# RWKV heads' transposes, inverse levels and chain outputs in fewer, larger steps, and working memory given back in smaller pieces

## The chip, the cores and the metric

The kernel runs on one core of a Trainium2 chip. The metric is the device time of one execution in microseconds; of a kernel, the median of its runs. The core has a matrix engine (TensorE, PE in the profile), a vector engine (VectorE, DVE), a scalar engine (ScalarE, ACT), GpSimd (POOL) and SyncE (SP), which run their own instruction streams and wait for one another by semaphores. SBUF is the working memory, PSUM holds what PE writes.

## What is computed

One layer of a decoder for 288 tokens (256 of a prompt, 8 sequences of 4 new tokens), all in float32:

```
h = RMSNorm_pre(x);  [p_rwkv | lru_x | lru_gate | q | k | v] = h @ W_in
y = concat(RWKV7(p_rwkv), RGLRU(lru_x, lru_gate), DilatedWindowAttn(q, k, v)) @ W_out
x = x + RMSNorm_post(y)
x = x + RMSNorm_post2(relu(RMSNorm_pre2(x) @ W1)^2 @ W2)
```

The width is 2048, the inner width of the feed-forward part 8192. RWKV7 has 8 heads of 64 with a matrix state, scanned along the tokens; the RG-LRU is a gated linear recurrence over 512 channels behind a convolution of width 4; the attention has 8 heads of 128 and, for the 32 new tokens, caches of keys and values of 2048 positions, of which 896 are used. The new states, keys and values are outputs too.

## The kernel before

**The weight stream.** All weights come as 380 chunks of 512 KB on SP's queue, into four slots (`w32`). Float32 precision is had by splitting: ACT rounds a chunk to its high half (`ring_h`, L393), DVE subtracts it and keeps the low half (`ring_l`, L394), into three slots each, and each product is three products of PE, high by high (L429), low by high (L430), high by low (L431), with 288 tokens as columns. These 128x288 products are called mains here. A chunk is 24 mains; the split of chunk i needs the slot of chunk i - 3. The chunks run in the order W_in (92 chunks, to about 480 us), W_out in four passes (32 chunks, to about 600 us), then the feed-forward part with 256.

**The other work.** RWKV, LRU and attention are written as Python generators in a list `gens`. After each chunk `pump(budget)` asks each generator for its next step, in the order of their priorities and of the list, until a budget is spent; a step that finds its operands missing yields nothing. A tile scheduler then places the step's instructions into each engine's stream. So on PE the main products of a chunk are interrupted by groups of small products of some step, and the list, the budget and the scheduler settle where.

**The generators of this change.** `gen_tok` (L786) transposes B, K and V of a half of the RWKV heads, `gen_mats` (L875) does the last doubling levels of the inverse of a triangular matrix, four heads at a time, `gen_chain` (L937) runs over the chunks of 64 tokens and updates the state Z, `gen_gn` (L1130) is the group norm, `gen_rwkv_sample` (L1027) does the new tokens, `gen_lru` (L1192) the recurrence, `gen_tables` (L1324) the position biases, `gen_sample_scores` (L1363), `gen_sample_soft` (L1431) and `gen_sample_pv` (L1458) the attention of the new tokens with the caches.

**The working memory.** `arena` hands out pieces of two SBUF tiles, `arx` and `ar1`; a generator that gets no piece yields and asks again. PE's small products write to five banks of PSUM (`banks`). The caches stream through `streams`, two buffers that are the halves of the tile `arm`. K loads (L1377, 1792 columns) and V loads (L1474, 2048 or 1536 columns) are issued on POOL's queue as soon as a buffer is free; `more_streams` (L359) adds up to two more buffers from the arena late in the phase. One V step takes two loads and has 28 products (L1496).

Of the kernel before, what the change touches and what calls it, by code (L numbers as in the profile page):

```python
# [11 lines left out]
AF = mybir.ActivationFunctionType  # L12
# [5 lines left out]
NT = NP_ + NS  # L18
# [293 lines left out]
def build(tc, A, O):  # L312
    nc = tc.nc
    sy, dv, ac, po, pe = nc.sync, nc.vector, nc.scalar, nc.gpsimd, nc.tensor
    with ExitStack() as ctx:
# [38 lines left out]
        arena = Arena([arx, ar1])  # L354
        facc = arm.rearrange("p (k t) -> p k t", k=KT)
        streams = [arm[:, 0:2304], arm[:, 2304:4608]]
# [186 lines left out]
        lora = arena.get(2, 512)  # L543
# [22 lines left out]
        def gen_prenorm():  # L566
# [12 lines left out]
            sy.dma_start(out=lora, in_=A["lora"].rearrange("p (a b) -> p a b", a=2))  # L579
# [81 lines left out]
        def gen_rwkv(hf):  # L661
# [6 lines left out]
            for f in range(2):  # L668
# [3 lines left out]
                pe.matmul(out=b0[:, :NT], lhsT=lora[0:64, 0, fs], rhs=mw[0:64], start=True, stop=True)  # L672
                pe.matmul(out=b1[:, :NT], lhsT=lora[64:128, 0, fs], rhs=mw[64:128], start=True, stop=True)
# [3 lines left out]
                yield 1.0  # L677
            half_up(LW, -0.5 * CDEC)
# [59 lines left out]
            gens.append(gen_tok(R, "B", BK[:, 0]))  # L738
            gens.append(gen_tok(R, "K", BK[:, 1]))
# [27 lines left out]
            gens.append(gen_tok(R, "V", MV))  # L767
# [18 lines left out]
        def gen_tok(R, name, src):  # L786
            for j in range(2):
                t = yield from aw(256, top=True)
                b, = yield from bk(1)
                for f in range(2):  # L790
                    pe.transpose(b[:, 128 * f:128 * f + 128], src[:, f, 128 * j:128 * j + 128], ident)
                ac.activation(out=t, in_=b[:, 0:256], func=AF.Copy)
                banks.put(b)
                R[name + str(j)] = t
                yield 0.25
# [79 lines left out]
        def gen_mats(hf, j):  # L875
            R = RS[hf]
            while "MA%d" % j not in R:
                yield 0
            MT = R["MA%d" % j]
            i64 = cbv("i64")  # L880
            i64b = i64.unsqueeze(1).to_broadcast([128, 4, 64])
# [4 lines left out]

            rc = (slice(0, 64), slice(64, 128))
# [5 lines left out]
            T, Q = R["TQ"][:, 4 * j:4 * j + 4], R["TQ"][:, 8 + 4 * j:12 + 4 * j]  # L893
            for l in range(4, 6):
                b, = yield from bk(1)
                for h in range(4):
                    for r in rc:
                        pe.matmul(out=v4(b)[r, h], lhsT=XT[r, h], rhs=T[r, h], start=True, stop=True)  # L898
                dv.tensor_tensor(out=Gp, in0=v4(b), in1=i64b, op=ALU.add)
                banks.put(b)  # L900
                if l < 5:
                    dv.tensor_tensor(out=XT, in0=MT[:, :, 0], in1=lvl(l + 1), op=ALU.mult)
                yield 0.65
# [4 lines left out]
                for h in range(4):  # L908
                    for r in rc:
                        if l < 5:  # L910
                            pe.matmul(out=v4(bT)[r, h], lhsT=Q[r, h], rhs=Gp[r, h], start=True, stop=True)
                        pe.matmul(out=v4(bQ)[r, h], lhsT=Gp[r, h], rhs=Q[r, h], start=True, stop=True)
                if l < 5:
                    ac.activation(out=T, in_=v4(bT), func=AF.Copy)
                    banks.put(bT)
                ac.activation(out=Q, in_=v4(bQ), func=AF.Copy)
                banks.put(bQ)
                yield 1.3 if l < 5 else 0.65
            arena.put(XT, Gp)
            while "V%d" % j not in R:  # L920
                yield 0
            VT = R["V%d" % j]
            AV = yield from aw(4, 64, top=True)
            b, = yield from bk(1)
            for h in range(4):
                e, f = h // 2, h % 2
                for r in rc:
                    pe.matmul(out=v4(b)[r, h], lhsT=MT[r, h, 1], rhs=VT[r, 128 * f + 64 * e:128 * f + 64 * e + 64],
                              start=True, stop=True)
            ac.activation(out=AV, in_=v4(b), func=AF.Copy)  # L930
            banks.put(b)
            arena.put(MT)
            yield 0.65
            R["AV%d" % j] = AV
            R["Q%d" % j] = Q

        def gen_chain(hf):  # L937
# [13 lines left out]
            for g in range(4):  # L951
# [7 lines left out]
                if g:  # L959
                    be = yield from bk(2)  # L960
                    for f in range(2):
                        for e in range(2):
                            re = slice(64 * e, 64 * e + 64)
                            pe.matmul(out=be[e][r, 64 * f:64 * f + 64], lhsT=AR[re, 0, f, tok], rhs=Z[re, f],
                                      start=True, stop=True)
                    for e in range(2):
                        dv.tensor_tensor(out=RH[r, 2 * e:2 * e + 2], in0=v2(be[e])[r], in1=AV[r, 2 * e:2 * e + 2], op=ALU.add)
                    banks.put(*be)
                    yield 0.35
# [38 lines left out]
                if g:  # L1008
                    bZ, = yield from bk(1)
                    for f in range(2):  # L1010
                        for e in range(2):
                            re = slice(64 * e, 64 * e + 64)
                            pe.matmul(out=bZ[re, 64 * f:64 * f + 64], lhsT=Z[re, f], rhs=AR[re, 1, f, tok],
                                      start=True, stop=True)
                    dv.tensor_tensor(out=yv, in0=v2(bZ), in1=yv, op=ALU.add)
                    banks.put(bZ)
# [836 lines left out]
```

## Time and profile before

| | |
|---|---|
| median of 3 runs | 1447.4 us (1447.09 to 1448.56) |
| profiled execution | 1447.71 us, of which the span is 1445.6 |
| mean granted clock of PE | 0.989 |
| PE busy | 1412.0 us, 98% of the span |
| DVE busy | 836.5 us, 58% |
| ACT busy | 600.2 us, 42% |
| POOL busy | 63.3 us, 4% |
| HBM | 190 GB/s over the span |

The span goes from the first to the last instruction of the trace. Busy time of PE is the time in which it has any product in flight; a group of small products among mains counts as busy like the mains themselves. The granted clock is the share of TensorE's full speed in a stretch; its two levels are 1.2 and 2.4 GHz. A wait is the idle time of an engine before an instruction, with what ended it.

### The profile page before, as it was taken

The numbers are of one execution on the slowest core, as the hardware profiler recorded it, in microseconds if no ns is written. First come the engines' busy times: TensorE is split into PE (matmuls) and PEld (weight loads), VectorE is DVE, ScalarE is ACT, GpSimd is POOL, SyncE is SP. The second block draws the span as 40 slices with busy tenths as digits, with TensorE's granted clock in tenths as the row PEclk, the third lists the DMA queues.
The fourth block names the chain that finished last, engine by engine and source line by source line (L and its number), as shares of the span: only waits on it lengthen the run. The fifth ranks groups of instructions, "written<-read, shape, count | busy, mean of one in ns | idle before, by whom it ended". The sixth has DMA issues, their size and how long they took to land.

```text
span 1445.6 us, 27979 instructions
## 1 busy us (share of the span) xinstructions
PE 1412.0 (98%) x11730; PEld 1340.2 (93%) x11730; DVE 836.5 (58%) x1431; ACT 600.2 (42%) x870; POOL 63.3 (4%) x127
## 2 busy tenths in 40 slices
PE   8999999899999999999999999999999999999995
PEld 8899778777878999999999999999999999999995
DVE  7796476645686756795533455544455444555555
ACT  7433422333352533664433344333344333444442
POOL 2101010210001100000000000000000000000000
PEclk9999999999999999999999999999999999999998
DMA  8546566676678774344444444444444445444442
GB/s 299 181 152 209 187 240 239 223 271 241 217 292 331 290 286 162 131 148 161 170 164 165 170 162 163 172 161 167 169 161 165 171 161 169 167 161 165 171 162 79
DMA packets 86047, 276.62 MB, mean 191 GB/s; under 512 B 22385, under 2 KB 26017, under 8 KB 83873
## 3 DMA queue, kind: packets, MB, share of 16 engines
q1 hardware_dynamic: 75136, 212.23, 42.6%
q0 software_dynamic: 9920, 60.83, 11.2%
q8 instruction: 92, 1.51, 0.4%
q10 hardware_dynamic: 864, 1.77, 0.4%
q14 instruction: 35, 0.28, 0.1%
HBM read 267.97 MB, written 6.84 MB: 190 GB/s over the span
## 4 chain that ended last, share of the span: by engine, by line
PE 82%; issue 7%; DMA 6%; DVE 4%; POOL 1%; ACT 0%; SPq 0%; POOLq 0%; DVEq 0%; ACTq 0%
PE mm L429 25%; PE mm L431 25%; PE mm L430 25%; DMA arm<-in_vc 2%; DMA arm<-in_kc 2%; PE bt L1409 1%; DVE ring_l L394 1%; PE bt L1496 1%; DMA ar<-in_vc 1%; DMA w<-in_w_in 0%; DVE arm L1830 0%; DMA do<-ar 0%; DVE arx L1831 0%; DVE hl L548 0%; PE bt L898 0%
## 5 line engine op out<-in xcount | busy, mean ns | idle before, releaser
L394 DVE TENSOR_TENSOR ring_l<-w,ring_h 128x1024 fp32r<-128x1024 f32 (+1 forms) x382 | 464.9, 1218 | 385.2 <-ACT ring_h L393 382.7
L393 ACT ACTIVATE ring_h<-w 128x1024 fp32r<-128x1024 f32 (+1 forms) x382 | 402.6, 1055 | 587.2 <-PE mm L430 538.9
L429 PE MATMUL mm<-hh,ring_h 128*128 128x288 f32 x1984 | 599.4, 302 | 4.6 <-ACT ring_h L393 2.8
L431 PE MATMUL mm<-hh,ring_l 128*128 128x288 f32 x1984 | 591.9, 299 | 1.3 <-DVE ring_l L394 1.3
L430 PE MATMUL mm<-hl,ring_h 128*128 128x288 f32 x1984 | 592.9, 299 | 0.0
L429 PEld LDWEIGHTS mm<-hh,ring_h 128*128 128x128 f32 x1984 | 373.6, 188 | 20.1 <-issue 11.8
L431 PEld LDWEIGHTS mm<-hh,ring_l 128*128 128x128 f32 x1984 | 374.9, 189 | 9.7 <-issue 4.3
L430 PEld LDWEIGHTS mm<-hl,ring_h 128*128 128x128 f32 x1984 | 374.6, 189 | 6.4 <-issue 3.5
L430 PE MATMUL mm<-fl,ring_h 128*128 128x288 f32 x1024 | 302.1, 295 | 0.0
L431 PE MATMUL mm<-fh,ring_l 128*128 128x288 f32 x1024 | 301.8, 295 | 0.0
L429 PE MATMUL mm<-fh,ring_h 128*128 128x288 f32 x1024 | 300.3, 293 | 0.0
L429 PEld LDWEIGHTS mm<-fh,ring_h 128*128 128x128 f32 x1024 | 192.5, 188 | 0.0
L430 PEld LDWEIGHTS mm<-fl,ring_h 128*128 128x128 f32 x1024 | 192.5, 188 | 0.0
L431 PEld LDWEIGHTS mm<-fh,ring_l 128*128 128x128 f32 x1024 | 192.4, 188 | 0.0
L1798 ACT ACTIVATE fh<-ft 128x288 fp32r<-128x288 f32 x64 | 28.3, 445 | 78.9 <-DVE ft L1797 78.9
L1806 DVE TENSOR_TENSOR arm<-mm,arm 128x288 f32<-128x288 f32 x48 | 22.0, 458 | 51.1 <-PE mm L431 51.1
L1799 DVE TENSOR_TENSOR fl<-ft,fh 128x288 fp32r<-128x288 f32 x64 | 29.2, 458 | 29.1 <-ACT fh L1798 29.1
L1409 PE MATMUL bt<-arm,ar 128*32 128x448 f32 x256 | 27.8, 546 | 1.7 <-DMA arm<-in_kc 1.7
L1797 DVE SCALAR_TENSOR_TENSOR ft<-mm,rt 128x288 f32<-128x288 f32 x63 | 28.3, 450 | 0.0
L1496 PE MATMUL bt<-arm,ar 128*32 128x128 f32 x648 | 22.6, 287 | 3.5 <-DMA arm<-in_vc 3.5
L1796 ACT ACTIVATE rt<-mm 128x288 f32<-128x288 f32 x63 | 24.9, 395 | 0.4 <-PE mm L431 0.4
L1496 PEld LDWEIGHTS bt<-arm,ar 128*32 128x32 f32 x648 | 17.8, 114 | 6.6 <-DVE ar L1290 3.7
(394 smaller groups left out, 898.6 us busy)
## 6 DMA issues: line engine op xcount, KB each, us to landing
w<-in_w SPq DMA_DIRECT2D x256, 512.0 KB
w<-in_w_in SPq DMA_DIRECT2D x91, 512.0 KB
arm<-in_kc POOLq DMA_DIRECT2D x32, 896.0 KB, 6.1
w<-in_w_out SPq DMA_DIRECT2D x32, 512.0 KB
arm<-in_vc POOLq DMA_DIRECT2D x15, 1024.0 KB, 6.8
ar<-in_vc POOLq DMA_DIRECT2D x9, 768.0 KB, 9.5
arm<-in_vc POOLq DMA_DIRECT2D x7, 768.0 KB, 7.0
arx<-in_xT SPq DMA_DIRECT2D x6, 576.0 KB
```

Source lines behind the costliest of these rows:

```text
L393: ac.activation(out=h[:, lo:hi], in_=t[:, lo:hi], func=AF.Copy)
L394: dv.tensor_tensor(out=l[:, lo:hi], in0=t[:, lo:hi], in1=h[:, lo:hi].bitcast(F32), op=ALU.subtract)
L429: pe.matmul(out=ps, lhsT=h, rhs=xh, start=start, stop=False)
L430: pe.matmul(out=ps, lhsT=h, rhs=xl, start=False, stop=False)
L431: pe.matmul(out=ps, lhsT=l, rhs=xh, start=False, stop=stop)
L1409: pe.matmul(out=bh[32 * h:32 * h + 32, 0:448], lhsT=qz[:, h, b], rhs=t[:, h], start=(b == 0), stop=(b == NB - 1))
L1496: pe.matmul(out=bb[32 * h:32 * h + 32, 0:128], lhsT=PT[:, kt, 32 * h:32 * h + 32], rhs=t[:, q, h], start=(kt == 0), stop=(kt == 6))
L1796: ac.activation(out=r, in_=ps, func=AF.Relu)
L1797: dv.scalar_tensor_tensor(out=f, in0=ps, scalar=0.0, in1=r, op0=ALU.max, op1=ALU.mult)
L1798: ac.activation(out=fh[:, m], in_=f, func=AF.Copy)
L1799: dv.tensor_tensor(out=fl[:, m], in0=f, in1=fh[:, m].bitcast(F32), op=ALU.subtract)
L1806: dv.tensor_tensor(out=facc[:, m], in0=ps, in1=facc[:, m], op=ALU.add)
```

## The change

- `gen_tok` transposes B and K in one step, with both token blocks, and V in one; before, there were two steps for each.
- `gen_mats` works on all eight matrices of a half (four heads of two token blocks) at once: a level has 16 products in a step where two generators had 8 each, and its DVE and ACT instructions are twice as wide.
- `gen_chain` takes the product of the state Z with the queries (bZ) in the step that makes the other product with Z, ACT copies it to the output Y, and DVE adds bU to it later. Before, ACT copied bU to Y and a step at the end of each chunk made bZ, which DVE added.
- `gen_tables` and the transposes of the softmax take two banks of PSUM at a time.
- Memory: the stream buffers have 2048 columns, the arena gets the remaining 512 of `arm`; the lora weights are two pieces, of which the first is freed early; AR and PC are freed after the chain, AV at its end as one piece; the LRU's output is four pieces that are taken when they are needed.
- `gen_lru` stands first in the list of generators, where it stood last.

```diff
--- before.py
+++ after.py
@@ -351,9 +351,9 @@
-        arena = Arena([arx, ar1])
+        arena = Arena([arx, ar1, arm[:, 4096:4608]])
         facc = arm.rearrange("p (k t) -> p k t", k=KT)
-        streams = [arm[:, 0:2304], arm[:, 2304:4608]]
+        streams = [arm[:, 0:2048], arm[:, 2048:4096]]
...
-        lora = arena.get(2, 512)
+        lora_in, lora_out = arena.get(512), arena.get(512)
...
-            sy.dma_start(out=lora, in_=A["lora"].rearrange("p (a b) -> p a b", a=2))
+            sy.dma_start(out=lora_in, in_=A["lora"][:, 0:512])
+            sy.dma_start(out=lora_out, in_=A["lora"][:, 512:1024])
...
+            if hf:
+                arena.put(lora_in, mw)
...
-            gens.append(gen_tok(R, "B", BK[:, 0]))
-            gens.append(gen_tok(R, "K", BK[:, 1]))
+            gens.append(gen_tok(R, ("B", BK[:, 0]), ("K", BK[:, 1])))
...
-        def gen_tok(R, name, src):
-            for j in range(2):
-                t = yield from aw(256, top=True)
-                b, = yield from bk(1)
-                for f in range(2):
-                    pe.transpose(b[:, 128 * f:128 * f + 128], src[:, f, 128 * j:128 * j + 128], ident)
-                ac.activation(out=t, in_=b[:, 0:256], func=AF.Copy)
...
+        def gen_tok(R, *pairs):
...
+            bs = yield from bk(len(pairs))
+            for i, ((name, src), b) in enumerate(zip(pairs, bs)):
+                for j in range(2):
+                    for f in range(2):
+                        o = 256 * j + 128 * f
+                        pe.transpose(b[:, o:o + 128], src[:, f, 128 * j:128 * j + 128], ident)
+                for j in range(2):
+                    t = R[name + str(j)] = ts[2 * i + j]
+                    ac.activation(out=t, in_=b[:, 256 * j:256 * j + 256], func=AF.Copy)
...
-        def gen_mats(hf, j):
+        def gen_mats(hf):
...
-            XT = yield from aw(4, 64, top=True)
-            Gp = yield from aw(4, 64, top=True)
-            dv.tensor_tensor(out=XT, in0=MT[:, :, 0], in1=lvl(4), op=ALU.mult)
+            XT = yield from aw(8, 64, top=True)
+            Gp = yield from aw(8, 64, top=True)
+            for j in range(2):
+                dv.tensor_tensor(out=XT[:, 4 * j:4 * j + 4], in0=MT[j][:, :, 0], in1=lvl(4), op=ALU.mult)
...
             for l in range(4, 6):
                 b, = yield from bk(1)
-                for h in range(4):
+                for h in range(8):
                     for r in rc:
-                        pe.matmul(out=v4(b)[r, h], lhsT=XT[r, h], rhs=T[r, h], start=True, stop=True)
-                dv.tensor_tensor(out=Gp, in0=v4(b), in1=i64b, op=ALU.add)
+                        pe.matmul(out=v8(b)[r, h], lhsT=XT[r, h], rhs=T[r, h], start=True, stop=True)
+                dv.tensor_tensor(out=Gp, in0=v8(b), in1=i64b, op=ALU.add)
...
+                    bZ, = yield from bk(1)
+                    for f in range(2):
+                        for e in range(2):
+                            re = slice(64 * e, 64 * e + 64)
+                            pe.matmul(out=bZ[re, 64 * f:64 * f + 64], lhsT=Z[re, f], rhs=AR[re, 1, f, tok],
+                                      start=True, stop=True)
...
+                    ac.activation(out=Y[:, :, tok], in_=v2(bZ), func=AF.Copy)
...
-                ac.activation(out=yv, in_=v2(bU), func=AF.Copy)
+                if g:
+                    dv.tensor_tensor(out=yv, in0=v2(bU), in1=yv, op=ALU.add)
+                else:
+                    ac.activation(out=yv, in_=v2(bU), func=AF.Copy)
...
-            arena.put(RH, U, Z, Zn)
+            arena.put(RH, U, Z, Zn, AR, PC)
...
-            S["LY"] = yield from aw(4, NT, top=True)
+            S["LY"] = []
...
-                    H = YT[4 + i] = S["LY"][:, i]
+                    H = YT[4 + i] = yield from aw(NT, top=True)
...
-                for lo, n in ((0, 464), (464, 464)):
-                    b, = yield from bk(1)
+                bs = yield from bk(2)
+                for b, lo, n in ((bs[0], 0, 464), (bs[1], 464, 464)):
...
-                yield 0.5
+            bs = yield from bk(2)
+            for kt in range(8):
+                n = 128 if kt < 7 else 32
+                pe.transpose(bs[kt // 4][0:n, 128 * (kt % 4):128 * (kt % 4) + 128], SS[:, g, 128 * kt:128 * kt + n], ident)
...
-        gens += [gen_tables(), gen_lora()]
+        gens += [gen_lru(), gen_tables(), gen_lora()]
         for hf in range(2):
-            gens += [gen_rwkv(hf), gen_form(hf), gen_inv(hf), gen_mats(hf, 0), gen_mats(hf, 1), gen_chain(hf), gen_gn(hf)]
-        gens += [gen_lru()]
+            gens += [gen_rwkv(hf), gen_form(hf), gen_inv(hf), gen_mats(hf), gen_chain(hf), gen_gn(hf)]
```

The order of instructions shows what this does. First PE, at about chunk 39 of the W_in phase, at the level that ends in L912 (L923 now): rows `x8` and `x16` are small products of `gen_mats`, the lines 429 to 431 are mains. Before:

```order
L429 MATMUL mm<-hh,ring_h 128x288
L912 MATMUL bt<-ar_88 64x64 x8
L430 MATMUL mm<-hl,ring_h 128x288
L431 MATMUL mm<-hh,ring_l 128x288
L429 MATMUL mm<-hh,ring_h 128x288
L430 MATMUL mm<-hl,ring_h 128x288
L912 MATMUL bt<-ar_88 64x64 x8
L431 MATMUL mm<-hh,ring_l 128x288
```

Now:

```order
L430 MATMUL mm<-hl,ring_h 128x288
L431 MATMUL mm<-hh,ring_l 128x288
L923 MATMUL bt<-ar_88 64x64 x16
L429 MATMUL mm<-hh,ring_h 128x288
L430 MATMUL mm<-hl,ring_h 128x288
L431 MATMUL mm<-hh,ring_l 128x288
```

Two interruptions of eight products have become one of sixteen. Over the W_in phase and the first passes of W_out the mains are interrupted 196 times before and 172 times now, by the same number of small products.

Second POOL's queue, from the second group of K loads (L1377, now L1392) to the V loads (L1474, now L1485); the name on the left is the tile which the buffer lies in. Before:

```order
L1377 DMA arm<-in_kc 128x1792 x10
L1474 DMA arm<-in_vc 128x2048
L1474 DMA arm<-in_vc 128x1536
L1474 DMA arm<-in_vc 128x2048
L1474 DMA arm<-in_vc 128x1536
L1474 DMA arm<-in_vc 128x2048
L1474 DMA arm<-in_vc 128x1536
L1474 DMA arm<-in_vc 128x2048
L1474 DMA arm<-in_vc 128x1536
L1474 DMA ar_88<-in_vc 128x2048
```

Now, with the first V loads ahead of it:

```order
L1485 DMA arm<-in_vc 128x1536
L1405 MEMSET ar_88 128x1024
L1485 DMA arm<-in_vc 128x2048
L1408 COPY ar_88<-arx 128x8x4 x4
L1485 DMA arm<-in_vc 128x1536
L1485 DMA ar_88<-in_vc 128x2048
L1558 DMA ar_88<-dtab 128x256 x2
L1558 DMA arx<-dtab 128x256 x2
L1392 DMA arm<-in_kc 128x1792 x10
L1047 DMA arx<-in_wkv 128x1024
L1392 DMA arm<-in_kc 128x1792 x6
L1485 DMA arm<-in_vc 128x1536
```

Five V loads stand ahead of the second group of K loads where two stood, and the buffers from the arena (`ar_88`, `arx`) come in from the fifth load, not the eleventh.

Third DVE, between two splits of weight chunks (L394). Before, the instructions between the splits of chunk 78 and 79 (chunks counted from 0):

```order
L1273 TENSOR_TENSOR ar1_88<-ar1_88,arx_83 128x288
L1150 RECIPROCAL ar1_88<-ar1_88 128x288
L1275 SCALAR_TENSOR_TENSOR ar1_88<-ar1_88,arx_83 128x288
L1150 RECIPROCAL ar1_88<-ar1_88 128x288
L1121 TENSOR_TENSOR ar1_88<-bt_84,ar1_88 128x512
L1151 TENSOR_TENSOR ar1_88<-ar1_88 128x576
L1123 TENSOR_TENSOR ar1_88<-ar1_88 128x512
L1154 TENSOR_SCALAR ar1_88<-ar1_88,pv_70 128x288 x2
L1115 TENSOR_TENSOR ar1_88<-ar1_88,ca_69 128x512
L1503 SCALAR_TENSOR_TENSOR arx_83<-bt_84,ca_69,arx_83 128x128
L1156 TENSOR_TENSOR ar1_88<-ar1_88 128x576
L394 TENSOR_TENSOR ring_l_81<-w32_3942,ring_h_80 128x1024
```

Now, those between chunk 81 and 82, first the beginning:

```order
L394 TENSOR_TENSOR ring_l_81<-w32_4054,ring_h_80 128x1024
L1278 TENSOR_SCALAR ar1_88<-ar1_88 128x288
L1153 SCALAR_TENSOR_TENSOR ar1_88<-bt_84,ar1_88 128x288
L1279 RECIPROCAL ar1_88<-ar1_88 128x288
L1304 TENSOR_TENSOR ar1_88<-ar1_88,pv_70 128x8
L1281 SCALAR_TENSOR_TENSOR ar1_88<-ar1_88 128x288
L1514 SCALAR_TENSOR_TENSOR arx_83<-bt_84,ca_69,arx_83 128x128
L1203 TENSOR_TENSOR ar1_88<-mm_4245,rs_in_72 128x288
L1286 TENSOR_SCALAR ar1_88<-ar1_88 128x288
L1287 TENSOR_TENSOR ar1_88<-ar1_88,arx_83 128x288
L1296 TENSOR_TENSOR arx_83<-arx_83,ar1_88 128x288 x2
L1299 SCALAR_TENSOR_TENSOR ar1_88<-ar1_88,arx_83 128x256
```

and the end:

```order
L1164 RECIPROCAL ar1_88<-ar1_88 128x288
L1135 TENSOR_TENSOR arx_83<-bt_84,arx_83 128x512
L1308 COPY arx_83<-ar1_88 128x8
L1165 TENSOR_TENSOR ar1_88<-ar1_88 128x576
L1137 TENSOR_TENSOR arx_83<-arx_83,arm_82 128x512
L1168 TENSOR_SCALAR ar1_88<-ar1_88,pv_70 128x288 x2
L1129 TENSOR_TENSOR ar1_88<-ar1_88,ca_69 128x512
L1170 TENSOR_TENSOR ar1_88<-ar1_88 128x576
L1514 SCALAR_TENSOR_TENSOR arx_83<-bt_84,ca_69,arx_83 128x128
L1310 SCALAR_TENSOR_TENSOR ar1_88<-ar1_88 128x288
L1305 TENSOR_TENSOR ar1_88<-ar1_88,arx_83 128x8
L394 TENSOR_TENSOR ring_l_81<-w32_4123,ring_h_80 128x1024
```

Between these two splits there are 45 other instructions now: the last steps of the LRU's first pair (L1278 to L1310), the group norm of the second half (L1153 to L1170), the sample state (L1129 to L1137) and evacuations.

## Rows read from the trace of the kernel before

**Rows 1.** The page: busy time, share of the span and instructions of each engine

```profile
PE 1412.0 (98%) x11730; PEld 1340.2 (93%) x11730; DVE 836.5 (58%) x1431; ACT 600.2 (42%) x870; POOL 63.3 (4%) x127
```

**Rows 2.** Windows: stretch; length, then busy time of each engine; clock, DMA

```profile
258.00:262.00 4.00, 4.00 (x17) 3.52 (x16) 3.12 (x8) 2.10 (x7) 0.00 (x0) 0.57 0.48 138
...
430.00:432.00 2.00, 0.00 (x0) 0.00 (x0) 1.82 (x4) 1.97 (x3) 0.00 (x0) 1.00 0.98 413
432.00:436.00 4.00, 2.57 (x35) 2.22 (x36) 1.71 (x5) 1.33 (x2) 0.53 (x1) 0.52 0.92 360
436.00:440.00 4.00, 4.00 (x41) 3.20 (x41) 0.73 (x4) 0.32 (x1) 0.47 (x1) 0.63 0.62 214
...
560.00:580.00 20.00, 20.00 (x153) 20.00 (x151) 12.69 (x19) 7.65 (x10) 0.00 (x0) 1.00 0.50 172
```

**Rows 3.** Waits of PE: who <- for what: us in total, times, longest

```profile
PE bt L1496 <- DMA arm<-in_vc: 3.5, 1, 3.5
...
PE bt L1409 <- DMA arm<-in_kc: 1.7, 1, 1.7
...
PE mm L431 <- DVE ring_l L394: 1.3, 4, 0.5
...
PE bt L1496 <- DMA ar<-in_vc: 1.1, 1, 1.1
PE bt L1421 <- DVE ar L1316: 1.0, 1, 1.0
```

**Rows 4.** Timeline of PE at 289 us, a step of 32 products: start, duration

```profile
289.40 0.29 PE L431 MATMUL mm<-hh,ring_l 128*128 128x288 f32 x1
...
290.74 0.40 PE L429 MATMUL mm<-hh,ring_h 128*128 128x288 f32 x1
290.98 0.30 PE L430 MATMUL mm<-hl,ring_h 128*128 128x288 f32 x1
```

**Rows 5.** Timeline of PE at 303 us, a step of 16 products

```profile
303.40 0.29 PE L429 MATMUL mm<-hh,ring_h 128*128 128x288 f32 x1
...
304.24 0.40 PE L430 MATMUL mm<-hl,ring_h 128*128 128x288 f32 x1
304.47 0.30 PE L431 MATMUL mm<-hh,ring_l 128*128 128x288 f32 x1
```

**Rows 6.** Timeline of DVE from 241 and from 401 us; in brackets idle before

```profile
241.53 1.23 DVE L394 TENSOR_TENSOR ring_l<-w,ring_h 128x1024 fp32r<-128x1024 f32 x1 [1.29 <-ACT ring_h L393]
...
256.38 1.21 DVE L394 TENSOR_TENSOR ring_l<-w,ring_h 128x1024 fp32r<-128x1024 f32 x1
...
401.46 1.22 DVE L394 TENSOR_TENSOR ring_l<-w,ring_h 128x1024 fp32r<-128x1024 f32 x1
...
407.12 1.95 DVE L1150 RECIPROCAL ar<-ar 128x288 f32<-128x288 f32 x1 [1.31 <-ACT ar L1146]
408.99 0.63 DVE L1121 TENSOR_TENSOR ar<-bt,ar 128x512 f32<-128x512 f32 x1
...
413.22 1.22 DVE L394 TENSOR_TENSOR ring_l<-w,ring_h 128x1024 fp32r<-128x1024 f32 x1
```

**Rows 7.** V loads (L1474), K loads (L1377) from issue; POOL's timeline

```profile
DMA to landing us min/median/max: 4.5/8.2/10.6
...
DMA to landing us min/median/max: 4.6/6.1/9.5
...
424.98 1.19 POOL L1474 DMA_DIRECT2D arm<-in_vc  x2 [11.37 <-PE bt L1496]
```

**Rows 8.** Groups of DVE by shape: line, form, count, busy us, mean ns

```profile
L1150 DVE RECIPROCAL ar<-ar 128x288 f32<-128x288 f32 x4 | 7.8, 1947 | 1.8 <-ACT ar L1146 1.8
...
L1290 DVE TENSOR_TENSOR ar<-ar,arx 128x8 f32<-128x8 f32 x16 | 2.2, 157 | 0.0
...
L1156 DVE TENSOR_TENSOR ar<-ar 128x576 f32<-128x576 f32 x2 | 1.5, 747 | 0.0
...
L1284 DVE TENSOR_TENSOR_SCAN ar<-ar,arx 128x256 f32<-128x256 f32 x2 | 1.3, 684 | 0.0
```

More of the change, by code (lines that the diff above doesn't have):

```diff
@@ L784, in gen_rwkv @@
             arena.put(MV)
-        def gen_tok(R, name, src):
-            for j in range(2):
-                t = yield from aw(256, top=True)
-                b, = yield from bk(1)
-                for f in range(2):
-                    pe.transpose(b[:, 128 * f:128 * f + 128], src[:, f, 128 * j:128 * j + 128], ident)
-                ac.activation(out=t, in_=b[:, 0:256], func=AF.Copy)
-                banks.put(b)
-                R[name + str(j)] = t
-                yield 0.25
+        def gen_tok(R, *pairs):
+            ts = []
+            for _ in range(2 * len(pairs)):
+                ts.append((yield from aw(256, top=True)))
+            bs = yield from bk(len(pairs))
[7 more added lines that the diff above has]
+                    ac.activation(out=t, in_=b[:, 256 * j:256 * j + 256], func=AF.Copy)
+            banks.put(*bs)
+            yield 0.5 * len(pairs)
         def v4(b):
@@ L873, in gen_inv @@
             R["TQ"] = TQ
-        def gen_mats(hf, j):
+        def gen_mats(hf):
             R = RS[hf]
-            while "MA%d" % j not in R:
+            while "MA1" not in R:
                 yield 0
-            MT = R["MA%d" % j]
-            i64 = cbv("i64")
-            i64b = i64.unsqueeze(1).to_broadcast([128, 4, 64])
+            MT = (R["MA0"], R["MA1"])
+            i64b = cbv("i64").unsqueeze(1).to_broadcast([128, 8, 64])
             def lvl(l):
@@ L1004, in gen_chain @@
                 yv = Y[:, :, tok]
-                ac.activation(out=yv, in_=v2(bU), func=AF.Copy)
+                if g:
+                    dv.tensor_tensor(out=yv, in0=v2(bU), in1=yv, op=ALU.add)
+                else:
+                    ac.activation(out=yv, in_=v2(bU), func=AF.Copy)
                 banks.put(bU)
                 yield 1.3
[L1008 to L1016, printed above, removed]
                 Z, Zn = Zn, Z
                 if c == 1:
-                    arena.put(MR, AV, BT, KTk, VT)
+                    arena.put(MR, BT, KTk, VT)
                     if j == 1:
-                        arena.put(R["TQ"])
+                        arena.put(R["TQ"], R["AV"])
             sy.dma_start(out=O["o_wkv_p"][:, 2 * hf:2 * hf + 2], in_=Z)
             yield 0.35
-            arena.put(RH, U, Z, Zn)
+            arena.put(RH, U, Z, Zn, AR, PC)
             R["Yp"] = True
@@ L1160, in gen_gn @@
                 b, = yield from bk(1)
[L1161 removed]
+                pe.matmul(out=b[:, :NT], lhsT=lora_out[:, 128 * fa:128 * fa + 128], rhs=S["sg"], start=True, stop=True)
                 dv.tensor_tensor(out=Y[:, f], in0=Y[:, f], in1=b[:, :NT], op=ALU.mult)
@@ L1167, in gen_gn @@
                 yield 0
-            arena.put(SQ, bv, R["AR"], R["PC"], R["PS"])
+            arena.put(SQ, bv, R["PS"])
             S["R%d" % hf] = True
             if hf:
-                arena.put(cb, lora, S["mw"], S["sg"], S["negs"], S["oneka"])
+                arena.put(cb, lora_out, S["sg"], S["negs"], S["oneka"])
         xbt, gbt = {}, {}
@@ L1676, in run_out @@
                 if n == "L":
-                    arena.put(S["LY"])
+                    arena.put(*S["LY"])
                 for hf in range(2):
```

74 lines of the change are left out of this document (36 added, 38 removed).

## The prediction, made before the changed kernel ran

> **What bounds the kernel now.** I read the busy shares first: PE works 1412.0 of 1445.6 us [rows 1], so its instruction stream is the clock of the program, and every other engine counts only where PE waits for it. A stretch that holds nothing but main products gives the price of one: 153 in 20.00 us, 0.131 us each [rows 2]. Then PE's waits, to see what the other 33 us hold: the longest is 3.5 us for a V-cache load, another V load costs 1.1, a K load 1.7, DVE's low-half split of a weight chunk (ring_l) 1.3 in four pieces, and a DVE result 1.0 [rows 3]. Last the windows around the two largest: in the 2 us from 430 PE does nothing, and in the next 8 us its granted clock is 0.52 and 0.63, a mix of 2.4 and 1.2 GHz; from 258 to 262, after PE has waited for DVE, it is 0.57 [rows 2]. An idle PE is thus paid for twice. The low clock costs the busy time by the missing share: 2.57 x 0.48 + 4.00 x 0.37 = 2.7 us after the V wait, and 4.00 x 0.43 = 1.7 us after the DVE wait.
>
> **Fewer, larger steps: a gain.** No product is removed: PE runs the same 9120 main products and the same other products, but the order of instructions shows 172 interruptions of the main products during the first two phases, where there were 196. So 24 interruptions go. What one costs beyond its own products is read from a group of 16 products and one of 32, all on 64x64 tiles. For 16: the last main before starts at 303.40, the second after at 304.47 [rows 5], 1.07 us, of which two mains would take 0.26: 0.81. For 32: 289.40 to 290.98 [rows 4], 1.58 us, less 0.26: 1.32. Sixteen more products thus cost 0.51, and 0.81 - 0.51 = 0.30 is the interruption. That is an upper end, as the two steps do not address their operands alike. The lower end is what the mains themselves show: the second main starts 0.23 us after the first, 304.24 to 304.47 [rows 5], against 0.131, so 0.10 us is lost at the return alone. Between 0.10 and 0.30 I take 0.20: 24 x 0.20 = 4.8 us gained (2.4 to 7.2). A fused step pays something back: it must wait for both its producers, and the next step of the chain follows only 7 or so main products (0.9 us) later, while the DVE addition and the ACT copies in between are twice as wide. The trace shows no such step; the nearest row is PE's wait of 1.0 us for a DVE result [rows 3]. With six fused levels in each of two halves, most of them covered by mains, I charge 0.8 us (0 to 2).
>
> **The V stream: a gain.** The two stream buffers shrink from 2304 to 2048 columns, which a V load just fills, and the smaller pieces freed early leave the arena room for the two extra stream buffers. Before, eight loads of the second V stretch go through the two buffers of `arm`, and only the ninth finds an arena piece; now five loads stand ahead of the second K group, and after it four buffers rotate, as POOL's order shows. A load lands 8.2 us after its issue in the median, 10.6 at most [rows 7]. With two buffers it can be issued only when PE has finished the step before: the one issued at 424.98 [rows 7] is what PE waits for until 433.4. With four, it is issued two steps ahead, and two steps with the mains between them take over 11 us. So both V waits go, 3.5 + 1.1 = 4.6 us, and the 2.7 us of low clock with them: 7.3. A POOL queue that issues earlier also moves its K loads: the first K load of group 1 needs a buffer which V now holds, and is issued about 30 mains and a V step (some 5 to 6 us) ahead of its use; it lands in 6.1 us in the median, 4.6 to 9.5 [rows 7]. That is a wait of 0 to 4 us where one of 1.7 was [rows 3]; I take 1.3, a gain of 0.4.
>
> Here the Trainium skill ("DMA: Bandwidth & Descriptors", section on the anatomy of one DMA) has a formula of 2.0 us and bytes over 436 GB/s, which gives 4.4 us for 1024 KB and 4.1 for 896 KB. By it the load of 424.98 would have landed at 429.4, before PE came, and the first K load would never be waited for, which would make the sum 1.3 us better. The trace disagrees: half of the V loads take 8.2 us or longer, with the weight stream on the same engines; I keep the measured times.
>
> **What hides at no cost.** The output product Z.AR moves up beside the other product of the chain; its copy to Y falls to ACT, and the addition to DVE, one instruction each as before. Both are off the chain that leads to the next Z. The split `lora` load is two DMAs on SP in place of one, at a time when nothing waits for lora. The four single LY tiles cost a name.
>
> **The new pile on DVE: a loss.** The generator of the LRU goes from the end of the list to its head, so its steps come at other places, and its last steps now meet the group norm of the second RWKV half and the sample state. Between DVE's split of chunk 81 and that of chunk 82 (counted from 0) now stand 45 other instructions. Their durations by rows of before: three reciprocals of 128x288 at 1.95 and two scans at 0.68 make 7.2 us; 13 of 128x8 at 0.157 make 2.0; the other 27, from 0.06 up to 0.75 us for the widest, add up to 10.9 [rows 8]. In all 20.2 us. Neighbours overlap by some 0.08 us (a reciprocal of 1.95 from 407.12, the next from 408.99 [rows 6]), so 20.2 - 45 x 0.08 + 1.1 for the split itself = 17.7 us from split to split, and up to 20 with two waits of 1.3 us for ACT's table loads, of the kind that stands at 407.12 [rows 6]. What can PE bear? Two piles of before tell. One from 401.46 to 413.22, 11.8 us, made PE wait for nothing. One from 241.53 to 256.38, 14.9 us [rows 6], made it wait some 1.6 us, 1.0 of it for L1316's result, 0.4 for the split and 0.2 for another [rows 3]. So some 13.3 us are free: three ring slots hold about that much PE work. The new pile exceeds this by 17.7 - 13.3 = 4.4 to 20 - 13.3 = 6.7 us; I take 5.5. As ends I keep 0 (if the two-engine schedule slips so that PE has more small work there; the V steps among the mains are such work) and 10 (if each wait for ACT is paid in full and PE is held at the V step as well). It can't gain, since nothing is removed there. After a wait of that size comes low clock, 1.7 to 2.7 us as worked out above; I take 2.2. The old pile at 241.53 stays in two parts of 11 and 9 us by the same rows; it is counted as unchanged.
>
> **Sum.** -4.8 + 0.8 - 7.3 - 0.4 + 5.5 + 2.2 = -4.0 us. The profiled run took 1447.7 us, 2.1 of them around its span of 1445.6; the median of the runs is 1447.4, 0.3 less. 1447.7 - 4.0 - 0.3 = 1443.4 us.
>
> **Rivals.** *The pile hides.* PE is itself late at that place, because the V steps and the GN products lie there, and DVE catches up: no stall, no low clock. Then -12 to -11 us, 1435.7. For it: the 11.8 us pile of before cost nothing. Against: the new one is half as long again. *The pile rules.* It costs 10 us, with 2.7 us of low clock, and the interruptions saved are worth only the 0.10 of their lower end: -2.4 + 0.8 - 7.3 - 0.4 + 10 + 2.7 = +3.4, 1450.8 us: slower. It decides from a pile of some 23 us between the splits, which the two ACT chains would have to stretch it to. For it: the LRU's last steps switch ACT tables against the group norm, so both wait for each other. Against: the rows give 20. *The V waits only move.* The change doesn't do what it says: four buffers, but their loads stand behind group 1's K loads in POOL's queue, so the first of them come as late as before. Then half of the 7.3 stays: 1447.0, no difference. For it: POOL issues in order, and six K loads stand between. Against: five V loads are ahead of them.
>
> **How the numbers follow.** The forecast has 0.48, with its own range of 1440.5 to 1446.5; the hidden pile 0.20, the ruling pile 0.17, the moved waits 0.15. A measurement of this kernel can tell some 0.2% from no change, 2.9 us. Faster by more, under 1444.5: two thirds of the forecast and the hidden pile, 0.33 + 0.20 = 0.53. Within: the rest of the forecast and most of the moved waits, 0.27. Slower: 0.20. The range reaches to the hidden pile's and the ruling pile's times, 1435.5 to 1450.5; beyond lie tails of about 1 in 10 each.
>
> **What would show it.** Right: no wait of PE for in_vc over 0.5 us, no low clock around 430; DVE's splits of chunks 81 and 82 some 18 to 20 us apart, PE waiting 4 to 7 us in that stretch (for the split, or for a step that stands behind the LRU's tail on DVE), and clock below 0.7 in the slice after it. Wrong: the two splits under 14 us apart; a K or V wait over 2 us; or a PE busy time, outside the low clock, that does not fall by about 5 us.

## The result, and the profile after

The changed kernel takes 1457.4 us in the median (1455.4 to 1463.4, four runs), the kernel before 1447.9 beside it: a ratio of 1.0075, with an interval of 1.0052 to 1.0098. It is slower by 9.5 us where 4 us less were forecast, and the time lies outside the range of 1435.5 to 1450.5. The profiled run took 1455.43 us, 7.7 more than that of before; it is the fastest of the four, so its trace shows rather too little of the loss than too much.

The page of the changed kernel, the rows that answer [rows 1]:

```profile
PE 1408.5 (97%) x11730; PEld 1340.2 (92%) x11730; DVE 834.6 (57%) x1427; ACT 596.7 (41%) x860; POOL 56.0 (4%) x127
```

PE works 3.5 us less than before, but in a span that is 8.1 us longer: it idles 11.6 us more. Its waits, the rows that answer [rows 3] (who <- for what: us in total, times, longest):

```profile
PE bt L908 <- DMA ar<-do: 10.5, 2, 9.0
PE bt L1268 <- DVE arx L1514: 3.7, 1, 3.7
...
PE bt L1424 <- DMA arm<-in_kc: 2.7, 3, 2.1
...
PE bt L1175 <- DVE arx L1514: 1.8, 1, 1.8
PE mm L431 <- DVE ring_l L394: 1.7, 3, 0.8
```

Both waits for in_vc are gone, as forecast. The first row is new in size: 9.0 us in one piece for `ar<-do`, the load of the diagonal inverses of the second RWKV half (the other 1.5 us are at the first half's step). Before, only the first half's step waited for this load:

```profile
PE bt L898 <- DMA ar<-do: 1.5, 1, 1.5
```

The second row was not foreseen either. The windows around the new waits, as [rows 2], show the low clock behind each (the third number from the end):

```profile
272.00:274.00 2.00, 2.00 (x16) 1.88 (x15) 1.87 (x8) 0.00 (x0) 0.00 (x0) 1.00 1.03 394
286.00:288.00 2.00, 1.50 (x7) 1.41 (x8) 0.00 (x0) 0.00 (x0) 0.00 (x0) 0.50 1.00 394
288.00:292.00 4.00, 4.00 (x30) 3.83 (x31) 1.23 (x1) 1.06 (x1) 0.00 (x0) 0.71 0.12 47
414.00:418.00 4.00, 1.28 (x3) 1.00 (x4) 2.46 (x4) 0.00 (x0) 0.00 (x0) 0.83 0.95 379
418.00:422.00 4.00, 4.00 (x26) 3.40 (x25) 2.39 (x3) 1.12 (x3) 0.00 (x0) 0.75 0.53 174
444.00:448.00 4.00, 4.00 (x16) 3.30 (x17) 3.07 (x8) 0.00 (x0) 0.00 (x0) 0.58 1.00 401
```

The loss of low clock, worked out as in the prediction, is 1.50 x 0.50 + 4.00 x 0.29 = 1.9 us from 286, 1.28 x 0.17 + 4.00 x 0.25 = 1.2 us from 414 and 4.00 x 0.42 = 1.7 us from 444.

**Where the 9 us come from.** `gen_inv` writes the inverses to a DRAM tile (`do<-ar`, L870 after, L863 before) and reads them back in another layout (`ar<-do`, L875, L868), both on SP's queue. SP's timeline after (start, duration, operation, idle before):

```profile
268.51 2.28 SPq L870 DMA_DIRECT2D do<-ar  x2
278.53 4.25 SPq L875 DMA_DIRECT2D ar<-do  x8
```

and before:

```profile
268.83 1.57 SPq L863 DMA_DIRECT2D do<-ar  x2
...
272.14 4.88 SPq L868 DMA_DIRECT2D ar<-do  x8
```

Before, the first load is issued 3.3 us after the store (268.83 to 272.14); after, 10.0 us (268.51 to 278.53). The chain of waits of the changed kernel (start, duration, what) says what ran in between:

```profile
269.18 9.22 DMA do<-ar
...
279.89 6.25 DMA ar<-do
...
286.50 0.44 PE bt L908 x2
```

The store takes 9.2 us, and the load that landed last takes 6.3. Two V loads, 1.8 MB, had been issued around the store, by POOL's timeline:

```profile
266.63 0.53 POOL L1485 DMA_DIRECT2D arm<-in_vc  x1 [1.11 <-PE bt L1507]
...
268.30 0.68 POOL L1485 DMA_DIRECT2D arm<-in_vc  x1
```

The first step of `gen_mats` (L908) comes to PE at 277.5 and stands there until 286.5. So PE is early as well: what it saves ahead of this place, and K steps that have moved behind it, bring it there 9.0 us after the issue of the store. Before, the step came at 283.0, 14.2 us after the issue, and didn't wait:

```profile
282.97 0.68 PE L898 MATMUL bt<-ar 64*64 64x64 f32 x16
```

The wait of 9.0 us is thus 5.2 us that PE comes sooner and 3.8 us by which the round trip, 18.0 us from the issue of the store to the step, is longer than the 14.2 that sufficed before.

**The second new wait.** DVE's timeline (in brackets its idle time before the instruction) and that of PE, both of the changed kernel:

```profile
414.21 0.46 DVE L1203 TENSOR_TENSOR arx<-mm,rs_in 128x288 f32<-128x288 f32 x1 [3.94 <-DMA o_conv_p<-arx]
...
423.33 1.23 DVE L394 TENSOR_TENSOR ring_l<-w,ring_h 128x1024 fp32r<-128x1024 f32 x1 [0.79 <-ACT ring_h L393]
...
442.30 1.21 DVE L394 TENSOR_TENSOR ring_l<-w,ring_h 128x1024 fp32r<-128x1024 f32 x1
```

```profile
416.72 1.32 PE L1268 MATMUL bt<-arx,ar 128*128 128x288 f32 x2 [3.66 <-DVE arx L1514]
...
437.77 0.40 PE L429 MATMUL mm<-hh,ring_h 128*128 128x288 f32 x1 [0.74 <-ACT ring_h L393]
...
441.99 0.75 PE L1175 MATMUL bt<-arm,ar 128*128 128x288 f32 x2 [1.81 <-DVE arx L1514]
```

DVE's evacuation of a gate (L1203) waits 3.94 us for the store of the convolution's last inputs, since it got the arena piece which that store still reads (shown by the second run below); the chain has the store itself:

```profile
406.93 7.19 DMA o_conv_p<-arx
```

PE's step of the LRU (L1268), behind it, waits 3.66. This store, too, stands beside V loads, issued at 405.25 and 405.91, and the DMA share from 408 to 414 is 0.95 to 1.02; that they stretched it is likely, but no run shows it. Then comes the pile that the prediction spoke of: the splits of chunks 81 and 82 stand at 423.33 and 442.30, 19.0 us apart, and PE waits 0.74 + 1.81 + 0.82 = 3.4 us there.

### The profile page after: what moved, and what is told of

It reads as the page before. It is cut to its first block, busy times and chain, and to the rows that moved or that the text cites. A ratio compares the mean times of both kernels' runs of the same rounds, so it can differ in the third digit from the quotient of the medians.

```text
span 1453.7 us, 27953 instructions
## 1 busy us (share of the span) xinstructions
PE 1408.5 (97%) x11730; PEld 1340.2 (92%) x11730; DVE 834.6 (57%) x1427; ACT 596.7 (41%) x860; POOL 56.0 (4%) x127
## 3 DMA queue, kind: packets, MB, share of 16 engines
q0 software_dynamic: 9920, 60.83, 11.4%
## 4 chain that ended last, share of the span: by engine, by line
PE 86%; DVE 5%; DMA 4%; issue 3%; ACT 1%; POOL 0%; SPq 0%; ACTq 0%; DVEq 0%; POOLq 0%
PE mm L429 26%; PE mm L430 26%; PE mm L431 26%; DMA arm<-in_kc 2%; PE bt L1424 1%; DVE ring_l L394 1%; PE bt L1507 1%; DMA do<-ar 1%; DMA w<-in_w_in 1%; ACT ring_h L393 1%; DMA o_conv_p<-arx 0%; DMA ar<-do 0%; DVE arm L1840 0%; DVE arx L1841 0%; DVE hl L548 0%
## 5 line engine op out<-in xcount | busy, mean ns | idle before, releaser
L394 DVE TENSOR_TENSOR ring_l<-w,ring_h 128x1024 fp32r<-128x1024 f32 (+1 forms) x382 | 465.1, 1218 | 407.4 <-ACT ring_h L393 398.9
L1392 POOL DMA_DIRECT2D arm<-in_kc x32 | 16.9, 529 | 133.2 <-PE bt L1424 112.1
L1715 DVE TENSOR_TENSOR ar<-mm,ar 128x288 f32<-128x288 f32 x32 | 14.5, 453 | 11.5 <-PE mm L431 11.4
```

What stands on the lines that cost most here:

```text
L394: dv.tensor_tensor(out=l[:, lo:hi], in0=t[:, lo:hi], in1=h[:, lo:hi].bitcast(F32), op=ALU.subtract)
L1392: after(po.dma_start(out=t, in_=A["kc"][seq[i]]), S["mark"])
```

## The experiments

The runs are numbered in the order in which they were made.

Theory A: the loss is made of waits at three places, two of them DMAs that the new places of the steps expose, and the low clock behind them; what the change was expected to gain is there. Theory B: the larger steps themselves cost PE's time, and a wait that is taken away comes back at the next step.

**The LRU back at the end of the list (first run).**

```diff
-        gens += [gen_lru(), gen_tables(), gen_lora()]
+        gens += [gen_tables(), gen_lora()]
...
+        gens += [gen_lru()]
```

> The changed kernel with the generator of the LRU put back to the end of the list, all else kept. Theory A (the loss is two waits for DMAs that the new places of steps expose, 9.0 us for the load of the inverses of the second RWKV half and 3.7 us for the store of the convolution's last inputs, the pile on DVE of 3.4 us, and the low clock behind each): the wait for the inverses stays, since that step keeps its place at main 1407; the wait for the store and the pile go, with their low clock: 3.7 + 1.4 + 3.4 + 1.7 = 10 us, 1457 to about 1447. Theory B (the larger steps themselves cost PE's time, and a wait taken away comes back at the next step): above 1454.

Measured: 1448.1 us, 1.0016 of before (0.9998 to 1.0033), as A has it. The waits of PE:

```profile
PE bt L908 <- DMA o_k<-arx: 9.2, 1, 9.2
...
PE mm L431 <- DVE ring_l L394: 2.3, 5, 0.7
```

The wait for the inverses is there in full. The profile puts it down to the o_k store, which is issued on SP's queue right behind the loads and landed last; the step needs the loads, and whether it waits for that store as well no run tells. The waits of the LRU's place are gone. That place accounts for 9.3 us of the changed kernel's time, as much as the whole loss against the kernel before: without it, what the inverses cost and what the change gains come out even.

**The arena piece given back later (second run).**

```diff
-                    arena.put(t)
                     yield 0
                     b0, b1 = yield from bk(2)
...
                     yield 1.0
+                    arena.put(t)
```

> The changed kernel, with the arena piece of the LRU's input given back one step later, so that the gate's evacuation doesn't get the piece that the store of the convolution's last inputs still reads. A: DVE no longer waits for that store: 3.7 us and about 1.4 of low clock, 1457 to about 1452; the pile between the splits of chunks 81 and 82 (21 us of DVE work by the same rows) and the wait for the inverses stay. B: no gain, PE waits as long for the next result of DVE.

Measured: 1453.7 us, 1.0052 (1.0032 to 1.0071): 3.8 us less than the changed kernel. The two intervals overlap, but each of its five runs is faster than each of the changed kernel's four, and in the trace DVE's gate evacuation and PE's step behind it no longer wait. The rest of the LRU's share, 1453.7 - 1448.1 = 5.6 us, fits the pile's 3.4 and its 1.7 of low clock; no run takes the pile away by itself.

**The store on another queue (third run).**

```diff
-                sy.dma_start(out=bass.AP(tensor=d.tensor, offset=d.offset + 8 * 256 * i, ...
+                ac.dma_start(out=bass.AP(tensor=d.tensor, offset=d.offset + 8 * 256 * i, ...
```

> The changed kernel, with the stores of the diagonal inverses issued on ACT's queue and not on SP's, behind three weight chunks. Nothing else moves by more than a few mains. If the 9.2 us of that store came from its place behind the weight chunks in SP's queue, it falls to about 3 us, as in the kernel before, the wait of 9.0 falls to about 3, and the time by some 7 us, to 1450. If it came from the DMA engines being shared with V loads and weights, the store stays at 7 to 9 us and the time at 1456 to 1458.

Measured: 1456.4 us, 1.0078 (1.0057 to 1.0100). The chain:

```profile
272.86 9.11 DMA do<-ar
```

From ACT's queue the store takes 9.1 us too. It was not the place behind three weight chunks in SP's queue. What stores on both queues share are the DMA engines and the memory behind them, which no run tells apart. Their windows from the store's issue on (the DMA share and GB/s are the last two numbers), first two of before, then one of the changed kernel, which had 0.72 in the two microseconds ahead of it and 1.03 in the two behind it (the row from 272 above):

```profile
268.00:270.00 2.00, 1.62 (x12) 1.19 (x9) 2.00 (x5) 1.49 (x3) 1.94 (x4) 1.00 0.52 105
270.00:272.00 2.00, 1.56 (x30) 1.18 (x34) 2.00 (x3) 0.48 (x2) 2.00 (x1) 1.00 0.63 192
...
270.00:272.00 2.00, 2.00 (x15) 1.79 (x14) 0.53 (x2) 1.46 (x2) 0.00 (x0) 1.00 0.99 365
```

**More slack (fourth run).** The step waits for its operands in the program by empty turns; five of them in place of three:

```diff
-            for _ in range(3):
+            for _ in range(5):
                 yield 0
             R["TQ"] = TQ
```

> The changed kernel, with five empty turns in place of three between the loads of the inverses and their first use. The first use in the second half moves from main 1407 to 1584; V and K steps move with it, and the largest pile on DVE falls from 21 to 12 us of work. A: the wait of 9.0 and its 1.9 of low clock go, and the pile's 3.4 + 1.7; the wait for the store may stay: 1457 - 16 = 1441, to 1447 with other waits. B: 1452 or more.

Measured: 1445.8 us, 0.9995 (0.9983 to 1.0008), 11.7 less than the changed kernel. The waits that are left:

```profile
PE bt L1424 <- DMA arm<-in_kc: 5.1, 3, 2.8
PE bt L1507 <- DMA arx<-in_vc: 4.6, 1, 4.6
```

The wait of 9.0 us is gone; 0.9 us for the inverses is left, at the first half's step. But V and K waits have come in its place, more than the forecast of 1441 had: the order of the cache loads has moved with the steps.

**The V loads held back (fifth run).**

```diff
                     if i < len(seq) and i not in vst:
+                        if i > 1 and "TQ" not in RS[1]:
+                            return
```

> The changed kernel, with the third and later V loads held back until the inverses of the second RWKV half have been loaded. A (the store of the inverses takes 9 us because V loads and weight chunks share the DMA engines with it): with those V loads gone from the stretch, the store takes 3 to 5 us, and the wait of 9 us falls to 3 or less. The V steps spread out by themselves and no pile over 9 us of DVE work is left after chunk 53, so the waits at chunks 78 to 82 go as well: 1457 - 8 - 10 = 1439, up to 1446 with new K waits. Rival: V loads have nothing to do with the store; then it still takes 9 us and the wait stays at 8 to 9: 1447 to 1450.

Measured: 1444.2 us, 0.9986 (0.9971 to 1.0001). The time came out as A has it, but not by the reason given. The store is as long as ever, and the wait is 10.1 us:

```profile
269.64 9.85 DMA do<-ar
...
291.42 0.44 PE bt L908 x2
```

POOL's timeline shows why: in the places of the V loads there are now K loads of the second group, of like size:

```profile
267.05 0.53 POOL L1392 DMA_DIRECT2D arm<-in_kc  x1 [1.08 <-PE bt L1509]
...
270.94 0.53 POOL L1392 DMA_DIRECT2D arm<-in_kc  x1
```

So the V loads were not the cause by being V loads. The gain comes from chunks 78 to 82: from 396 to 452 us PE waits 0.2 us in all, at full clock.

**Weights alone (ninth run).** The K loads of the second group held back as well, by two lines more in the other generator:

```diff
                     if i < len(seq) and i not in kst:
+                        if i > 15 and "TQ" not in RS[1]:
+                            return
```

> The changed kernel, with the third and later V loads and the K loads of the second group held back until the inverses of the second half have been loaded, so that between 262 and 286 us the store and the loads of the inverses share the DMA engines with weight chunks alone. If the cache loads, whichever they are, stretch the store, it takes 3 to 5 us in place of 9, and the wait of 9 us falls to 4 or less. If the three weight chunks ahead of it do it, it stays at 8 to 9 us and the wait as well. The time says little, since the K loads come late.

Measured: 1457.7 us, 1.0078 (1.0056 to 1.0101). The chain:

```profile
271.23 3.88 DMA do<-ar
...
276.61 10.45 DMA ar<-do
```

The store falls to 3.9 us, with the weight chunks still ahead of it on SP's queue (and two loads of 128 KB beside it). So cache loads, of either kind, are what stretched it. The wait of PE did not fall below 4, though, as expected: it is 7.9 us. The loads that had been held back were issued in the same microseconds as the loads of the inverses, and those now take 10.5 in place of 6.3:

```profile
275.86 0.54 POOL L1489 DMA_DIRECT2D ar<-in_vc  x1 [3.32 <-DVE ar L1582]
276.39 1.06 POOL L1394 DMA_DIRECT2D arm<-in_kc  x2
```

The round trip has two halves on the DMA engines, and 1.8 to 2.8 MB of cache meet one or the other.

**The streams on the kernel before (sixth run).**

```diff
-        arena = Arena([arx, ar1])
+        arena = Arena([arx, ar1, arm[:, 4096:4608]])
-        streams = [arm[:, 0:2304], arm[:, 2304:4608]]
+        streams = [arm[:, 0:2048], arm[:, 2048:4096]]
```

> The kernel before, with stream buffers of 2048 columns and the other 512 columns of that tile given to the arena, nothing else. The same 196 interruptions; a third V buffer is found at the fifth load, a fourth at the tenth. By the prediction's term for V the waits of 3.5 and 1.1 us and 2.7 us of low clock go: 1447.1 - 7 = 1440. If the V waits only move to other loads: 1445 to 1448.

Measured: 1449.6 us, 1.0022 (1.0009 to 1.0035). No gain; the waits for V have moved to other loads, and two waits for DVE have come:

```profile
PE bt L1496 <- DMA arm<-in_vc: 4.0, 3, 2.3
...
PE bt L777 <- DVE ar L857: 1.9, 1, 1.9
...
PE bt L1254 <- DVE arx L1503: 1.6, 1, 1.6
```

So the V gain of the changed kernel, which its trace shows, is not this edit's alone. In this run two V loads stand ahead of the second K group, as before, where the changed kernel has five; that this is what was lacking, no run shows. The low clock around 430 is gone here (1.00 from 424 to 444), and the time did not fall even so.

**Still more slack (seventh run).** Six empty turns:

```diff
-            for _ in range(3):
+            for _ in range(6):
```

> The changed kernel, with six empty turns between the loads of the inverses and their first use. The first use in the second half moves to main 1626, the V loads return behind the second K group, the piles on DVE are 10 and 12 us of work. A: no wait for the inverses, and K and V waits of under 2 us together: 1441 to 1445. B (waits only move): 1448 or more.

Measured: 1435.9 us, 0.9927 (0.9912 to 0.9942): faster than both kernels, and below what A expected. Its waits:

```profile
PE bt L1424 <- DMA arm<-in_kc: 4.8, 3, 2.7
PE bt L1574 <- DVE arx L1578: 3.0, 1, 3.0
...
PE bt L1507 <- DMA ar<-in_vc: 1.0, 1, 1.0
...
PE bt L908 <- DMA ar<-do: 0.2, 1, 0.2
```

The wait for the inverses is 0.2 us, at the first half's step, and none in the second. The store is not faster for it: from its issue to the first load pass 8.4 us, but the step now comes later.

```profile
294.77 1.28 SPq L870 DMA_DIRECT2D do<-ar  x2
...
303.13 5.29 SPq L875 DMA_DIRECT2D ar<-do  x8
```

More than that wait has gone, since the steps behind it move too: the waits at chunks 78 to 82 are away as well. Between the profiled runs of the changed kernel and of this one PE idles 45.2 - 31.4 = 13.8 us less and is busy 1408.5 - 1401.9 = 6.6 us less; the low clock behind the changed kernel's three waits is 4.8 us.

**Three causes away at once (eighth run)**: the V loads held back, `range(5)`, and the LRU last, by the edits shown above.

> V loads held back as in the fifth run, five empty turns before the use of the inverses, and the LRU's generator at the end of the list: all three suspected causes away at once. A: the gains alone are left, 4 us of interruptions and about 7 of V waits: 1436 to 1442. B: 1446 or more.

Measured: 1443.3 us, 0.9977 (0.9965 to 0.9989); a V wait of 4.6 us and a K wait of 4.2 stand in the way of the 1436 to 1442.

Then two variants of the version with six turns. The LRU last, by the first edit above (tenth run):

> The seventh run's kernel with the LRU's generator at the end of the list. The seventh has no pile over 13 us of DVE work and no wait of PE for the LRU, so its place in the list should no longer matter: within 3 us of 1436. If the place of the LRU is worth something by itself, it shows here as 5 us or more either way.

Measured: 1436.7 us, 0.9928 (0.9901 to 0.9955): as expected, the place of the LRU has no value of its own. This run and the first differ only in the three empty turns more, both with the LRU last. Between them lie 1448.1 - 1436.7 = 11.4 us, which is what the first run's wait of 9.2 us and some 2 us of low clock behind it (0.50 and 0.60 from 284 to 292) come to. It is the closest that the runs come to the price of this wait alone; other steps move with the turns here too.

And the streams as before, the edit of the sixth run the other way round (eleventh run):

```diff
-        arena = Arena([arx, ar1, arm[:, 4096:4608]])
+        arena = Arena([arx, ar1])
-        streams = [arm[:, 0:2048], arm[:, 2048:4096]]
+        streams = [arm[:, 0:2304], arm[:, 2304:4608]]
```

> The seventh run's kernel with the stream buffers of 2304 columns and without the 512 columns for the arena. If the V term of the prediction holds (7 us for two more buffers in time), V waits of 3 to 5 us come back and the time is 1440 to 1444. If what mattered for V were other pieces given back early, the time stays at 1436 and V waits stay at 1 us.

Measured: 1439.8 us, 0.9954 (0.9932 to 0.9977), with V waits of 2.9 us. The streams may thus be worth 3 to 4 us here, half of the V term, but the intervals of this run and the seventh touch, and on the kernel before they were worth nothing.

On the theories: A has the three places right. B is right in that a wait taken away can come back at another step, as in the fourth and eighth runs; that larger steps cost PE's time, no trace shows.

**The price of an interruption by itself (twelfth run).** In the feed-forward part, where only mains run, small products are put into the W2 product of each of its four blocks:

```diff
+                    for i in range(groups.get(k, 0)):
+                        r = slice(64 * (i % 2), 64 * (i % 2) + 64)
+                        last = pe.matmul(out=bx[r, 64 * (i // 2 % 8):64 * (i // 2 % 8) + 64], lhsT=ident[r, r],
+                                         rhs=rs_in[r, 0:64], start=True, stop=True)
...
+                      ({}, {2: 16}, {2: 8, 5: 8}, {2: 32})[j])
```

> The seventh run's kernel, with idle small products of 64x64 put into the second products of the feed-forward part, where nothing else interrupts the main products. Its four blocks have 32 chunks each: in the first nothing is added, in the second 16 small products in one place of each chunk, in the third twice 8 in two places, in the fourth 32 in one place. The output is not changed. Third less second is 32 times the price of one interruption: by the prediction 0.20 us, 6.4 us, with ends of 3.2 (only the return, 0.10) and 9.6 (0.30). Fourth less second is 512 small products: by 0.032 us each 16 us. If an interruption had no price, third and second would be equal.

The windows are the four blocks (length; then busy times; the clock is 1.00 in all):

```profile
702.49:804.03 101.54, 101.54 (x770) 101.54 (x769) 40.05 (x34) 39.16 (x49) 0.00 (x0) 1.00 0.51 166
906.43:1048.73 142.30, 142.30 (x1795) 134.84 (x1793) 46.92 (x49) 34.70 (x34) 0.00 (x0) 1.00 0.37 121
1151.13:1304.30 153.17, 153.17 (x1794) 138.31 (x1793) 46.91 (x49) 34.70 (x34) 0.00 (x0) 1.00 0.35 113
1406.69:1578.72 172.03, 172.03 (x2817) 164.57 (x2816) 49.71 (x61) 45.69 (x62) 0.00 (x0) 1.00 0.26 84
```

Third less second: 153.17 - 142.30 = 10.9 us, over 32 chunks 0.34 us for one interruption more, a little over the upper end of 0.30. Fourth less second is 29.7 us, not 16: each of these small float32 products stands in the trace as two matmuls (an 8 of the order is an x16 of the timeline), so it is 1024 matmuls of 0.029 us. This is one run of the kernel.

## Why the prediction was wrong, step by step

**The step that failed is a wait that the sum put at next to nothing.** The part on larger steps said that a fused step must wait for both its producers, took PE's wait of 1.0 us for a DVE result as the nearest row, and charged 0.8 us. The producer that counted is not DVE but a round trip through DRAM of some 18 us. The waits of before have a row for exactly this load, 1.5 us of L898 for `ar<-do` at the first half's step, and it did not go into the rows that I rested on. It measured 9.0 us in the second half, and 1.9 of low clock behind it, where 0.8 us (0 to 2) were charged. Nor is it the fusing that made it: PE comes to the step 5.2 us sooner after the store's issue, and the V loads, which the sum counted as gain alone, lengthen the round trip by at least 3.8. By itself this turns the forecast's gain of 4.0 us into a loss of 6.1 (-4.0 - 0.8 + 10.9); the store in the next paragraph adds 4.9.

**"What hides at no cost" left out the DMAs that read memory which is given back earlier.** With the LRU first in the list, its step gives the arena piece back while a store still reads it. It cost 3.7 us and 1.2 of low clock; the second run, 3.8 us faster, shows it.

**The V stream was right in the changed kernel**: no wait for in_vc, and no low clock around 430. Its mechanism was told too simply: the two buffers alone gain nothing on the kernel before, and at most some 4 us on the best version. What the early loads collide with, the store of the inverses, was not asked. The fifth and ninth runs show that any cache load does it.

**The K loads** were taken as 0.4 us better and are 1.0 worse: 2.7 us against 1.7 [rows 3]. The longest, 2.1 us, is over the 2 us that the prediction itself named as a sign of being wrong.

**The pile on DVE was right**: 19.0 us from split to split, where 17.7 to 20 were worked out, and waits of 3.4 us and 1.7 of low clock where 5.5 and 2.2 were charged. The 13.3 us that PE can bear were too few by some 2. That three ring slots hold that much PE work does not follow from the rows: 72 mains of 0.131 us are 9.4.

**The interruptions** were worth more each, 0.34 us in place of 0.20. Of 24 x 0.34 = 8.2 us the changed kernel shows less: PE's busy time less the low clock in it goes from 1412.0 - 2.7 - 1.7 = 1407.6 to 1408.5 - 1.9 - 1.2 - 1.7 = 1403.7 us, 3.9 us, close to the forecast's 4.8 less 0.8. Where the other 4 us are, no run here settles: the 24 are of several shapes, and the price is that of 64x64 products.

**The sum again**, with what was measured: interruptions and what fusing pays back -3.9, V -7.3, K +1.0, the pile 3.4 + 1.7, the inverses 9.0 + 1.9, the store of the convolution 3.7 + 1.2, and the low clock at 258, 1.7 us, which the changed kernel's profiled run does not show: +9.0 us. Measured are 7.7 between the two profiled runs. The rest are waits of under 1 us that come and go.

**The rivals.** "The pile rules" ended on the right side, by luck: it charged 10 us of waits and 2.7 of low clock to the pile, which cost 3.4 and 1.7. No rival had a DMA in it that gets late because another comes early.

## What to carry to other kernels

When a change makes one engine's transfers earlier, list every small transfer that someone waits for in that stretch, above all round trips through DRAM, and price them with the engines full. A step that PE reaches sooner has less time for its operands: compare the time from the issue of the load to its first use before and after, in order and in microseconds. And when memory is given back sooner, look for the store that still reads it.

## What was not expected of the hardware

Two stores of 64 KB took at most 3.3 us at a DMA share of 0.52 to 0.63, 3.9 behind three weight chunks without cache loads, and 9.1 to 9.9 with 1.8 MB of cache loads issued beside them, whether they were issued on SP's queue or on ACT's. Waits of 0.4 + 0.6 + 0.6 us at the same three products, around 254 us, were followed by full clock in the profiled run of the changed kernel and by 0.50 from 256 to 258 in that of the second experiment, which gives PE the same instructions up to there: here the low clock after the same short waits differs from run to run.
